# Matrix multiply with GELU on one core: a new contraction order for 32-element transpose reads, narrower transfers of B, and four row tiles of A per opening load

## The chip, the cores and the metric

The kernel runs on one core of one Trainium2 chip. The metric is the device time of one execution in microseconds (us). All runs quoted here are fast (mean granted clock 0.99 to 1.0). The times "before" in the experiments are runs of the kernel before on the same chip, in turn with the kernel under test; experiments of different calls ran on different chips, and each call has its own "before". A ratio is the mean time of one kernel's fast runs over the mean of the other's fast runs of the same rounds, so it isn't quite the ratio of the medians that stand beside it.

## The reference

```python
# a: 4096 x 4096 float32, b: 4096 x 4096 float32, output float32
x = np.matmul(a, b)
return 0.5 * x * (1 + np.tanh(np.sqrt(2 / np.pi) * (x + 0.044715 * x**3)))
```

The kernel multiplies in bf16 and accumulates in float32.

## The kernel before

A contraction of 4096 is cut into four chunks of 1024. The matmuls here take A with the contraction on the partitions (the first dimension of the kernel's tiles), so A is loaded with a cast to bf16 into a staging tile, and VectorE transposes it (one instruction of 128 x 1024, 1.98 us; the index maps below are written for blocks of 32 x 32):

```python
a_v = a.rearrange("(t mb mm) (c g r) -> t c g mm mb r", mb=4, mm=Q, g=4, r=RUN)   # Q=32, RUN=256
b_v = b.rearrange("(c p j) n -> c p j n", p=P, j=NJ)                              # P=128, NJ=8
...
def load_a(t, c):
    if c == 0:
        at[t] = at_pool.tile([P, NKT, P], BF16, name="aT", tag="aT")
    s = stage_pool.tile([P, 4, RUN], BF16, name="a16", tag="a16")       # bufs=8
    for g in range(4):
        nc.gpsimd.dma_start(out=s[g * Q : (g + 1) * Q, :, :], in_=a_v[t, c, g])
    src = s.rearrange("p mb (q j) -> p j mb q", j=NJ)
    dst = at[t][:, c * NJ : (c + 1) * NJ, :].rearrange("p j (mb q) -> p j mb q", mb=4)
    nc.vector.transpose(dst, src)
```

Partition p of B holds rows 8p to 8p+7 of a chunk, so B goes in one transfer over 128 partitions, and the transpose reads its source with a step of 8 elements. The opening works on four row tiles and two column blocks (eight accumulators) while the data arrive:

```python
for c in range(NCHK):                       # 4 chunks
    for i in range(H):                      # 4 row tiles
        load_a(i, c)                        # four transfers of 64 KB (bf16)
        for n in range(2):
            load_b(n, c, 2 * i, 2 * i + 2)  # one transfer of 256 KB each
... # 256 matmuls on these; then row tiles 4 to 7, then all other column blocks
```

After that B comes 1 MB at a time and A tile by tile, ahead of their use. GpSimd issues all loads, which also cast float32 to bf16 (260.05 MB are read from HBM, 130.06 MB are moved by their queue); SyncE issues the stores. The order in which GpSimd issues the loads is not always that of the program: in the trace of this kernel, 44 loads of A for the second eight row tiles, which the program has behind all column blocks of B, are issued from 147.7 to 209.6 us, ahead of column block 5.

## Time and profile before

| | before |
|---|---|
| time, median of 3 runs | 1799.44 us (1799.33 to 1801.78) |
| matmuls, spacing after 90 us | 8192, 0.2158 us (0.21583) |
| tensor engine's lost time: start of the last weight load less 8191 x 0.21583 | 26.1 us, all in the first 90 us |
| transposes | 128 of 1.98 us |
| opening: last packet of A and B starts at | 75.6 us |
| opening: weight load 257 starts at | 80.1 us |

The trace has one weight load, reading a 128 x 128 block of A, for each of the 8192 matmuls. Weight loads are all recorded, so the start of the 257th tells when the opening's 256 matmuls are through, and packet records tell when its 12.58 MB (counted in bf16) are. From 90 us on TensorE paces everything: no two weight loads are more than 0.22 us apart. The times of weight loads in the prediction were read 0.25 us too early against the timeline's clock; here they stand on that clock (80.1 for its 79.9).

### The profile page before, as it was taken

The page shows a single profiled execution, that of the slowest core. Times are in us where ns is not written, and L with a number is a line of the kernel's source. Part 1 is how long each engine was busy: PE and PEld are TensorE (multiplying, and loading weights), DVE is VectorE, ACT ScalarE, POOL GpSimd, SP SyncE. Part 2 cuts the span into 40 slices and gives each one's busy share as a digit, 9 for nine tenths or more (in the row PEclk, how much of TensorE's full clock was granted, in tenths as well). Part 3 has the DMA queues.
Part 4 walks back from the last instruction along what each step waited for, and adds up shares of the span by engine and source line. Part 5 has one row for each costly group of instructions (what it writes and reads, how often), then busy time and mean ns, then how long its engine had stood idle before and what let it go on. Part 6 is the DMA issues. An engine that isn't in the chain of part 4 may idle for free.

```text
span 1798.2 us, 18458 instructions
## 1 busy us (share of the span) xinstructions
PE 1765.6 (98%) x8029; PEld 801.5 (45%) x8192; DVE 248.7 (14%) x128; ACT 153.8 (9%) x257; POOL 371.5 (21%) x632
## 2 busy tenths in 40 slices
PE   7899999999999999999999999999999999999999
PEld 2344444444444444444444444444444444444444
DVE  3450300006700000000850000000090000000000
ACT  0000000000000000000000000000000000000000
POOL 8751520005810000000680000000070000000000
PEclk9999999999999999999999999999999999999999
DMA  9999994416954666520795446661090654566101
GB/s 166 193 173 223 174 190 90 98 41 95 151 104 88 129 131 134 101 70 36 115 146 113 97 97 129 135 129 42 35 135 35 135 105 87 107 135 129 42 35 42
DMA packets 206737, 198.38 MB, mean 110 GB/s; under 512 B 14144, under 2 KB 173888, under 8 KB 206656
## 3 DMA queue, kind: packets, MB, share of 16 engines
q0 software_dynamic: 169792, 130.06, 49.2%
q1 hardware_dynamic: 36864, 67.13, 10.5%
q8 instruction: 64, 1.05, 0.2%
q14 instruction: 17, 0.14, 0.0%
HBM read 260.05 MB, written 67.11 MB: 182 GB/s over the span
## 4 chain that ended last, share of the span: by engine, by line
PE 94%; DMA 3%; POOL 2%; issue 1%; DVE 0%; ACT 0%; DVEq 0%; ACTq 0%; POOLq 0%
PE acc L74 94%; DMA Bc<-in_b_dram 2%; POOL a L59 1%; DMA a<-in_a_dram 1%; POOL Bc L68 0%; DVE aT L62 0%; ACT y L81 0%; DVEq L62 0%; ACTq L81 0%; POOLq L163 0%; POOLq L59 0%
## 5 line engine op out<-in xcount | busy, mean ns | idle before, releaser
L74 PE MATMUL acc<-Bc,aT 128*128 128x512 bf16 x8029 | 1765.6, 379 | 29.0 <-DMA Bc<-in_b_dram 18.2
L74 PEld LDWEIGHTS <-aT 128*128 128x128 bf16 x8192 | 801.5, 98 | 992.6 <-issue 16.1
L62 DVE STREAM_TRANSPOSE aT<-a 128x1024 bf16<-128x1024 bf16 x128 | 248.7, 1983 | 1101.6 <-PE acc L74 965.1
L59 POOL DMA_DIRECT2D a<-in_a_dram x512 | 275.9, 553 | 452.4 <-DVE aT L62 348.1
L81 ACT ACTIVATE y<-acc 128x512 f32<-128x512 f32 x256 | 152.5, 597 | 1640.7 <-PE acc L74 1573.9
L68 POOL DMA_DIRECT2D Bc<-in_b_dram x116 | 96.0, 836 | 808.7 <-PE acc L74 593.5
L81 ACT ACT_TABLE_LOAD x1 | 1.3, 1283 | 0.7 <-PEq L163 0.7
L163 POOL MEMSET const-float32-0.0<- 128x1 f32 x1 | 0.1, 98 | 0.2 <-issue 0.2
L163 POOL MEMSET const-bfloat16-1.0<- 128x1 bf16 x1 | 0.1, 101 | 0.0
L163 POOL MEMSET const-float32-1.0<- 128x1 f32 x1 | 0.1, 98 | 0.0
L163 POOL MEMSET const-uint8-127<- 128x1 uint8 x1 | 0.1, 98 | 0.0
## 6 DMA issues: line engine op xcount, KB each, us to landing
Bc<-in_b_dram POOLq DMA_DIRECT2D x84, 1024.0 KB, 19.5
out_dram<-y SPq DMA_DIRECT2D x256, 256.0 KB, 2.1
a<-in_a_dram POOLq DMA_DIRECT2D x512, 64.0 KB, 4.0
Bc<-in_b_dram POOLq DMA_DIRECT2D x32, 256.0 KB, 5.6
```

The source lines that it names most:

```text
L59: nc.gpsimd.dma_start(out=s[g * Q : (g + 1) * Q, :, :], in_=a_v[t, c, g])
L62: nc.vector.transpose(dst, src)
L68: nc.gpsimd.dma_start(out=bc[n][:, c * NJ + j0 : c * NJ + j1, :], in_=b_v[c, :, j0:j1, n * NC : (n + 1) * NC],)
L74: nc.tensor.matmul(acc[:, :], at[t][:, kt, :], bc[n][:, kt, :], start=(kt == 0), stop=(kt == NKT - 1),)
L81: nc.scalar.activation(y[:, :], acc[:, :], ACT.Gelu_apprx_tanh)
L163: nc = _bacc.Bacc("TRN2", target_bir_lowering=False, num_devices=1)
```

## The change

Its intent is that transposes read runs of 32 adjacent elements. For that, row q of a 32-partition group g must be contraction index 256g + 32j + q, which no longer lets B go in one transfer over 128 partitions. B is split in four, and the opening's A is loaded for four row tiles at once.

```diff
-    a_v = a.rearrange("(t mb mm) (c g r) -> t c g mm mb r", mb=4, mm=Q, g=4, r=RUN)
-    b_v = b.rearrange("(c p j) n -> c p j n", p=P, j=NJ)
+    a_v = a.rearrange("(x mm) (c g r) -> c g mm x r", mm=Q, g=4, r=RUN)
+    b_v = b.rearrange("(c g j q) n -> c g q j n", g=4, j=NJ, q=Q)
...
-    def load_a(t, c):
+    def load_a(t0, nt, c):
...
-        s = stage_pool.tile([P, 4, RUN], BF16, name="a16", tag="a16")
+        s = stage_pool.tile([P, 4 * nt, RUN], BF16, name="a16", tag=f"a16_{nt}", bufs=2 if nt > 1 else 3)
         for g in range(4):
-            nc.gpsimd.dma_start(out=s[g * Q : (g + 1) * Q, :, :], in_=a_v[t, c, g])
-        src = s.rearrange("p mb (q j) -> p j mb q", j=NJ)
+            nc.gpsimd.dma_start(
+                out=s[g * Q : (g + 1) * Q, :, :], in_=a_v[c, g, :, 4 * t0 : 4 * (t0 + nt), :]
+            )
+        for t in range(t0, t0 + nt):
...
+            src = s[:, 4 * (t - t0) : 4 * (t - t0 + 1), :].rearrange("p mb (j q) -> p j mb q", j=NJ)
...
     def load_b(n, c, j0, j1):
-        nc.gpsimd.dma_start(
-            out=bc[n][:, c * NJ + j0 : c * NJ + j1, :],
-            in_=b_v[c, :, j0:j1, n * NC : (n + 1) * NC],
-        )
+        for g in range(4):
+            nc.gpsimd.dma_start(
+                out=bc[n][g * Q : (g + 1) * Q, c * NJ + j0 : c * NJ + j1, :],
+                in_=b_v[c, g, :, j0:j1, n * NC : (n + 1) * NC],
+            )
...
     for c in range(NCHK):
-        for i in range(H):
-            load_a(i, c)
+        load_a(0, H, c)
+        for j in range(0, NJ, 4):
             for n in range(2):
-                load_b(n, c, 2 * i, 2 * i + 2)
+                load_b(n, c, j, j + 4)
```

More of the change, by code (lines that the diff above doesn't have):

```diff
@@ L45 @@
     psum_pool = ctx.enter_context(tc.tile_pool(name="psum", bufs=8, space=bass.MemoryType.PSUM))
-    a_v = a.rearrange("(t mb mm) (c g r) -> t c g mm mb r", mb=4, mm=Q, g=4, r=RUN)
-    b_v = b.rearrange("(c p j) n -> c p j n", p=P, j=NJ)
+    a_v = a.rearrange("(x mm) (c g r) -> c g mm x r", mm=Q, g=4, r=RUN)
+    b_v = b.rearrange("(c g j q) n -> c g q j n", g=4, j=NJ, q=Q)
     at = {}
     bc = {}
-    def load_a(t, c):
-        if c == 0:
-            at[t] = at_pool.tile([P, NKT, P], BF16, name="aT", tag="aT")
-        s = stage_pool.tile([P, 4, RUN], BF16, name="a16", tag="a16")
+    def load_a(t0, nt, c):
+        s = stage_pool.tile([P, 4 * nt, RUN], BF16, name="a16", tag=f"a16_{nt}", bufs=2 if nt > 1 else 3)
         for g in range(4):
-            nc.gpsimd.dma_start(out=s[g * Q : (g + 1) * Q, :, :], in_=a_v[t, c, g])
-        src = s.rearrange("p mb (q j) -> p j mb q", j=NJ)
-        dst = at[t][:, c * NJ : (c + 1) * NJ, :].rearrange("p j (mb q) -> p j mb q", mb=4)
-        nc.vector.transpose(dst, src)
+            nc.gpsimd.dma_start(
+                out=s[g * Q : (g + 1) * Q, :, :], in_=a_v[c, g, :, 4 * t0 : 4 * (t0 + nt), :]
+            )
+        for t in range(t0, t0 + nt):
+            if c == 0:
+                at[t] = at_pool.tile([P, NKT, P], BF16, name="aT", tag="aT")
+            src = s[:, 4 * (t - t0) : 4 * (t - t0 + 1), :].rearrange("p mb (j q) -> p j mb q", j=NJ)
+            dst = at[t][:, c * NJ : (c + 1) * NJ, :].rearrange("p j (mb q) -> p j mb q", mb=4)
+            nc.vector.transpose(dst, src)
     def new_b(n):
@@ L139 @@
                 for c in range(NCHK):
-                    load_a(x, c)
+                    load_a(x, 1, c)
             else:
```

## The prediction

> **What bounds the kernel now.** I read the page first, for the share of each engine, then the tensor engine's idle time, then the first 90 us instruction by instruction.
>
> ```profile
> span 1798.2 us, 18458 instructions
> ...
> PE 1765.6 (98%) x8029; PEld 801.5 (45%) x8192; DVE 248.7 (14%) x128; ACT 153.8 (9%) x257; POOL 371.5 (21%) x632
> ...
> L74 PE MATMUL acc<-Bc,aT 128*128 128x512 bf16 x8029 | 1765.6, 379 | 29.0 <-DMA Bc<-in_b_dram 18.2
> L62 DVE STREAM_TRANSPOSE aT<-a 128x1024 bf16<-128x1024 bf16 x128 | 248.7, 1983 | 1101.6 <-PE acc L74 965.1
> L59 POOL DMA_DIRECT2D a<-in_a_dram x512 | 275.9, 553 | 452.4 <-DVE aT L62 348.1
> L68 POOL DMA_DIRECT2D Bc<-in_b_dram x116 | 96.0, 836 | 808.7 <-PE acc L74 593.5
> ```
>
> PE is busy 98% and idle only 29.0 us, most of it behind B's transfers. The 8192 weight loads (all recorded) give the pace: from 90 us to the end they start 0.2158 us apart with no gap over 0.25 us. So 8192 x 0.2158 = 1768 us is a floor that this change doesn't touch, and 2% faster than 1799.44 would be 1763.5, below that floor. After the last weight load (1793.75) come 4.4 us of matmul, GELU and store, also untouched. What can move is the opening: the weight load numbered 294 starts at 89.5 us, where 294 x 0.2158 = 63.5 would do, so 26 us are lost there. The timeline shows how:
>
> ```profile
> 8.22 0.59 PE L74 MATMUL acc<-Bc,aT 128*128 128x512 bf16 x1 [8.22 <-DMA Bc<-in_b_dram]
> ...
> 72.07 2.00 DVE L62 STREAM_TRANSPOSE aT<-a 128x1024 bf16<-128x1024 bf16 x1 [3.11 <-DMA a<-in_a_dram]
> 74.31 14.40 PE L74 MATMUL acc<-Bc,aT 128*128 128x512 bf16 x65 [0.67 <-DMA Bc<-in_b_dram]
> ...
> 89.78 20.46 PE L74 MATMUL acc<-Bc,aT 128*128 128x512 bf16 x92 [1.06 <-DVE aT L62]
> ```
>
> The columns are start, length, engine and operands, and what ended the idle time. VectorE's last transpose of the four opening tiles ends at 74.07; 27 of the opening's 256 matmuls are left then and the opening ends at 79.9 (weight load 257). Row tile 4 then arrives too slowly and PE waits twice more, at 84.9 and 87.9 us, 2 us together by the spacing of the weight loads.
>
> ```profile
> 20.00:30.00 10.00, 9.44 (x43) 4.00 (x41) 5.29 (x3) 0.00 (x0) 8.40 (x15) 1.00 1.28 184
> 50.00:60.00 10.00, 8.71 (x39) 3.83 (x40) 5.68 (x3) 0.00 (x0) 8.76 (x15) 1.00 1.25 187
> 100.00:110.00 10.00, 9.95 (x47) 4.50 (x47) 7.95 (x5) 1.14 (x2) 8.11 (x16) 1.00 0.99 135
> ```
>
> ```profile
> POOL a L59 <- DMA Bc<-in_b_dram: 61.9, 25, 5.7
> ```
>
> The first rows are of the table by stretch: length, then busy time of PE, weight load, VectorE, ScalarE and GpSimd, granted clock, DMA share, GB/s. In the opening the DMA engines are over-full (shares above 1: packets overlap) at 184 to 187 GB/s of bf16. It needs 4.19 MB of A and 8.39 MB of B: 12.58 MB at 187 is 67 us; with the first packet at 2.8 us, some dips and about 1.5 us of landing that is the 74 us seen. Each contraction chunk starts 17 us after the one before it (weight loads 65, 129, 193 at 27.4, 44.2, 61.3) for 64 x 0.2158 = 13.8 us of matmul. **The transfers bound the opening, PE bounds the rest.** The single line, from the list of waits, is GpSimd waiting to issue: by count of the issues each such wait is for the transfer issued eight earlier, so I take eight to be in flight at most.
>
> [...] The old transpose steps 8 bf16[...]. The trace has 1.98[...]. [...] A already goes in 32-partition transfers: I counted packets in 0.4 us steps of the opening, and steps with almost only A (512 B packets, 60 ns) move a median of 179 GB/s, steps with almost only B (1 KB, 98 ns) 197. [...] a loss of some per cent for B is possible. [...] The trace shows 0.43 us steps up to 17 us and 0.216 after; the later opening gaps, at most 2.2 us, cost no clock.
>
> **The change part by part.**
> 1. Transposes, 128 of them: [...] VectorE idles 1101 us; on the path lies only the time from landing to use in each opening chunk[...] and it counts only where A lands last.
> 2. B's order and split: the same 1 KB packets, 94,208 of them. Issues rise from 116 to 64 + 336 = 400. GpSimd's cost of one depends weakly on its descriptors (0.72 us for 256, 0.87 for 1024, 0.55 for A's 128): I take 0.55 for the opening's and 0.6 for the later. B is then 35 + 200 = 235 us against 96. Opening A is 16 issues at about 0.65, 10 us for the old 64 x 0.55 = 35. GpSimd in all: 371 - 35 + 10 - 96 + 235, about 485 us, 27% busy. In an opening chunk it is 16 x 0.55 + 4 x 0.65 = 11.4 us, inside 17 us of transfer. Eight transfers of 128 KB still are 1 MB in flight, 5.5 us of transfer.
> 3. Opening order. A chunk is now: A of all four tiles (1.05 MB, 5.6 us at 187), then B's first half for column blocks 0 and 1 (2.8 us each), then the second halves. With chunk 3's data starting near 2.8 + 3 x 17.2 = 54.4, A has landed at 61.5 and the first B piece near 64.6 (with 1.5 us of landing). If the instructions are ordered to use pieces as they come, as those of before are, each piece is 3.45 us of matmul for 2.8 us of transfer, and PE runs through: 64.6 + 13.8 = 78.4. If both column blocks must be there before it starts, 81.3. Before it was 79.9. I take 79.
> 4. Row tile 4: its loads queue directly behind B and have three staging buffers of their own, with faster transposes to free them. Three chunks should be there by 80, so I expect most of the 2 us of waits to go. Old 79.9 + 2.0 = 81.9 against new 79 + 0.5 = 79.5: 2.4 us less.
> 5. A new cost: the 3.4 us of slack per chunk, before spread over three gaps, becomes one gap. [...] 0.8 us.
>
> Sum: 1799.4 - 2.4 + 0.8 = 1797.8.
>
> **The rivals.** *B's narrow transfers are slower.* If all opening traffic ran at A's 179 instead of 187, 12.58 MB would take 70.3 us, 3 us more: 1801. [...] against it: the A steps reach 192 in their best tenth though their packets are half the size. *Block 2 of B becomes late.* It is first needed at weight load 513, 136.6 us, its last chunk 5.2 us later; in the trace its transfer starts at 116.8 and 4.19 MB at 200 GB/s last 21 us, so only some 3 us are spare. Slower issue of tiles 4 to 7 (64 x 0.55 = 35 us at least, before 44) with three staging buffers instead of eight could delay it: 2 to 5 us more, 1800 to 1803. Against it: those 44 us contain waits, and the transposes free the buffers sooner. *Something large:* GpSimd, blocked at a staging buffer, holds back B later on. It waits 348 us for VectorE in before without hurting PE; B has 55 us for 22 us of transfer, so I give this a few per cent only. *The faster transposes are the gain:* [...] Against it: chunks queue behind transfers, so only the last counts.
>
> **Range and chances.** The rivals span 1794 to 1803; I take 1794.5 to 1802 and 1797.8. Over 2% faster needs less than the floor: 0.005. Over 2% slower is 36 us more, which only a blocked B or halved bandwidth gives: 0.03.
>
> **What would show it.** [...] GpSimd near 27%; weight load 257 at 78 to 81 us; no PE gap over 0.3 us after 82; weight loads at 0.2158 apart. Opening stretches under 180 GB/s would speak for the narrow transfers; 0.43 us steps at a chunk's start for the clock; a gap near 137 to 142 for late B. PE gaps in mid-run, or transposes still near 2 us, would make the prediction wrong.

## The result, and the profile after

The changed kernel took 1796.05 us (median of 4 runs, 1795.03 to 1797.56) against 1800.16 us for the kernel before (4 runs). The ratio is 0.9977, with a 95% interval of 0.9959 to 0.9994: 4 us less, far within 2%. A repeat gave 1795.89 us and a ratio of 0.9976.

These lines are from the changed kernel's page: the shares of the engines, then the groups of instructions with busy time, mean duration and idle time before them.

```profile
span 1793.3 us, 18949 instructions
...
PE 1773.7 (99%) x8192; PEld 802.3 (45%) x8192; DVE 157.1 (9%) x128; ACT 153.8 (9%) x257; POOL 477.4 (27%) x868
...
L78 PE MATMUL acc<-Bc,aT 128*128 128x512 bf16 x8192 | 1773.7, 380 | 15.9 <-DMA Bc<-in_b_dram 14.5
L72 POOL DMA_DIRECT2D Bc<-in_b_dram x400 | 226.8, 571 | 818.0 <-PE acc L78 635.7
L57 POOL DMA_DIRECT2D a<-in_a_dram x464 | 250.4, 547 | 345.0 <-DVE aT L65 288.6
...
L65 DVE STREAM_TRANSPOSE aT<-a 128x1024 bf16<-128x1024 bf16 x128 | 157.1, 1239 | 1200.3 <-PE acc L78 686.1
```

TensorE's listed idle time fell from 29.0 to 15.9 us, but these two can't be compared: 163 matmul records are missing before and none after, and 8.3 of the 29.0 us lie after 92 us, where no two weight loads are more than 0.22 us apart. The weight loads give the fair figure below. The transposes are 0.74 us shorter each, and GpSimd issues 864 transfers instead of 628. The timeline of the changed kernel shows how the opening ends (start, length, engine, what ended the idle time):

```profile
58.75 4.62 DVE L65 STREAM_TRANSPOSE aT<-a 128x1024 bf16<-128x1024 bf16 x4 [11.20 <-DMA a<-in_a_dram]
...
63.43 46.52 PEld L78 LDWEIGHTS <-aT 128*128 128x128 bf16 x217 [0.80 <-DVE aT L65]
63.43 46.79 PE L78 MATMUL acc<-Bc,aT 128*128 128x512 bf16 x216 [0.31 <-DVE aT L65]
```

The last chunk's four transposes run in a row, and from 63.43 us TensorE never stops again. Weight load 257 starts at 76.4 us, 3.7 us earlier than the 80.1 before. The wait behind row tile 4 (weight load 295 came at 89.8 us, 1.65 us after the one before it) is gone too, which is the rest, 1.2 us, of the 5.0 us by which the lost time fell in the profiled runs (26.1 to 21.2). The mid-run pace is 0.2158 us, as before. So all of the difference lies in the opening, and the next view says where it comes from: the table by stretch for 4 to 58 us, first of the kernel before, then of the changed one (length, busy time of PE, weight load, VectorE, ScalarE and GpSimd, granted clock, DMA share, GB/s).

```profile
4.00:58.00 54.00, 42.55 (x172) 17.41 (x176) 23.91 (x12) 0.00 (x0) 45.77 (x77) 1.00 1.25 181
```

```profile
4.00:58.00 54.00, 42.38 (x173) 17.71 (x173) 13.87 (x12) 0.00 (x0) 37.26 (x67) 0.97 1.30 193
```

The same bytes flow at 193 GB/s instead of 181, and GpSimd is busy for 8.5 us less. The last opening packet starts at 70.7 us instead of 75.6. Not all of that lies in this stretch: the kernel before also had a dip to 96 and 28 GB/s from 65 to 67 us, after GpSimd stood still for 1.7 us for a reason that the profile doesn't show. The changed kernel has such a pause too (2.4 us before 60.5 us), and then a dip to 98 GB/s. The prediction had taken this rate as fixed at 187.

### The profile page after: what moved, and what is told of

Same layout as the page of the kernel before. It is cut to its first block, busy times and chain, and to the rows that moved or that the text cites. A ratio compares the mean times of both kernels' runs of the same rounds, so it can differ in the third digit from the quotient of the medians.

```text
span 1793.3 us, 18949 instructions
## 1 busy us (share of the span) xinstructions
PE 1773.7 (99%) x8192; PEld 802.3 (45%) x8192; DVE 157.1 (9%) x128; ACT 153.8 (9%) x257; POOL 477.4 (27%) x868
## 3 DMA queue, kind: packets, MB, share of 16 engines
q8 instruction: 64, 1.05, 0.2%
## 4 chain that ended last, share of the span: by engine, by line
PE 96%; DMA 2%; POOL 1%; issue 0%; DVE 0%; ACT 0%; DVEq 0%; ACTq 0%; POOLq 0%
PE acc L78 96%; DMA a<-in_a_dram 1%; POOL Bc L72 1%; POOL a L57 0%; DMA Bc<-in_b_dram 0%; DVE aT L65 0%; ACT y L85 0%; DVEq L65 0%; ACTq L85 0%; POOLq L167 0%
## 5 line engine op out<-in xcount | busy, mean ns | idle before, releaser
L78 PE MATMUL acc<-Bc,aT 128*128 128x512 bf16 x8192 | 1773.7, 380 | 15.9 <-DMA Bc<-in_b_dram 14.5
L72 POOL DMA_DIRECT2D Bc<-in_b_dram x400 | 226.8, 571 | 818.0 <-PE acc L78 635.7
L57 POOL DMA_DIRECT2D a<-in_a_dram x464 | 250.4, 547 | 345.0 <-DVE aT L65 288.6
L65 DVE STREAM_TRANSPOSE aT<-a 128x1024 bf16<-128x1024 bf16 x128 | 157.1, 1239 | 1200.3 <-PE acc L78 686.1
```

The lines of the kernel that those rows point to most:

```text
L72: nc.gpsimd.dma_start(out=bc[n][g * Q : (g + 1) * Q, c * NJ + j0 : c * NJ + j1, :], in_=b_v[c, g, :, j0:j1, n * NC : (n + 1) * NC],)
L78: nc.tensor.matmul(acc[:, :], at[t][:, kt, :], bc[n][:, kt, :], start=(kt == 0), stop=(kt == NKT - 1),)
```

## The experiments

Theory I says that the stream was slow before because A came in transfers of 64 KB, which GpSimd issues too slowly to keep the DMA engines full. Theory W says that the new order's addresses or the narrow transfers made the stream faster. Theory V says that the short transposes made the gain. "Wide" B means transfers over 128 partitions, "narrow" over 32. What GpSimd can issue is also limited in number: in the traces each issue comes after the landing of the transfer eight earlier (at least 0.28 us after it, for all 620 issues that have one in the kernel before and all 856 in the changed kernel). No run changes that limit of eight, so it is part of theory I here and not a theory of its own. Each edit is against the changed kernel unless it says otherwise. All results were correct.

### Old contraction order, narrow B (e1_old_order_narrow_b)

```diff
-            src = s[...].rearrange("p mb (j q) -> p j mb q", j=NJ)
+            src = s[...].rearrange("p mb (q j) -> p j mb q", j=NJ)
-    b_v = b.rearrange("(c g j q) n -> c g q j n", g=4, j=NJ, q=Q)
+    b_v = b.rearrange("(c g q j) n -> c g q j n", g=4, j=NJ, q=Q)
```

Expected:

> The changed kernel with the old contraction order (transposes step 8 elements, 1.98 us each) but with its loads: A of four row tiles at once, B in 32-partition transfers. If the size of the opening's A transfers is what counts (theory I: GpSimd's issue and the eight in flight kept the DMA engines short of work before), the opening's last packet starts at about 71 us as in the changed kernel (before: 75.6) and the time is 1796 to 1798. If the addresses of the new order make the transfers faster (theory W), it starts at 75 and the time is 1799 to 1801. If the transposes are the gain (theory V), the last packet starts near 71 but weight load 257 comes 3 to 4 us later than the 76.4 us of the changed kernel, and the time is 1799 to 1800.

Measured: 1797.44 us (before: 1800.42), ratio 0.9984 (0.9970 to 0.9997). The last opening packet starts at 70.5 us, weight load 257 at 80.2. The timeline of this run shows the cost of the long transposes in the last chunk:

```profile
59.57 7.64 DVE L65 STREAM_TRANSPOSE aT<-a 128x1024 bf16<-128x1024 bf16 x4 [8.26 <-DMA a<-in_a_dram]
...
67.26 2.70 PEld L78 LDWEIGHTS <-aT 128*128 128x128 bf16 x14 [1.76 <-DVE aT L65]
```

This is its stretch from 4 to 58 us:

```profile
4.00:58.00 54.00, 38.34 (x159) 16.02 (x163) 22.85 (x12) 0.00 (x0) 36.99 (x66) 1.00 1.29 192
```

The stream is as fast as in the changed kernel (192 GB/s against 193), so theory W's addresses fall. Four transposes in a row take 7.64 us here and 4.62 us in the changed kernel, and TensorE waits for the fourth until 67.3. That is where theory V is right in part: the new order is worth 1797.44 - 1796.0 = 1.4 us, given that A arrives four tiles at once (1796.0 stands for the changed kernel's 1796.05 and 1795.89. They were run at other times. Their intervals overlap with this run's). Theory V's other mark, weight load 257 later by 3 to 4 us, was met by the profiles, 80.2 against 76.4, but these are of this kernel's slowest run (1798.87) and the changed kernel's fastest (1795.03); in the changed kernel's other profile, below, it is at 78.0.

### Old contraction order, wide B (e2_old_order_wide_b)

The edit is the one above, and B's load is put back to one transfer over 128 partitions:

```diff
+    b_v = b.rearrange("(c p j) n -> c p j n", p=P, j=NJ)
-        for g in range(4):
-            nc.gpsimd.dma_start(out=bc[n][g * Q : (g + 1) * Q, ...], in_=b_v[c, g, :, ...])
+        nc.gpsimd.dma_start(out=bc[n][:, ...], in_=b_v[c, :, ...])
```

Expected:

> As the run with the old order and narrow B, but B in 128-partition transfers of 512 KB in the opening and 1 MB later, as before. Theory I: last opening packet at 69 to 71 us, GpSimd under 50% busy in the opening, 1795 to 1797. If the narrow transfers themselves were the gain (another form of theory W), the packet starts at 75 and the time is 1799 to 1801. Theory V: 1799 to 1800 by late transposes. Against the run with narrow B it gives the price of the split: within 1 us by theory I.

Measured: 1795.87 us (before: 1800.42), ratio 0.9976 (0.9963 to 0.9988), last opening packet at 68.0 us. This is the same stretch, 4 to 58 us, of this run:

```profile
4.00:58.00 54.00, 39.85 (x167) 16.70 (x171) 22.87 (x12) 0.00 (x0) 21.45 (x32) 1.00 1.32 201
```

With neither the new order nor the split, this kernel is as fast as the changed one. GpSimd is busy 21 us of 54, and the stream runs at 201 GB/s. Set beside the run with narrow B, the split costs 1797.44 - 1795.87 = 1.6 us, a little more than was allowed for. The five runs of each don't overlap (1795.18 to 1796.57, 1797.09 to 1798.87), so this cost is shown. So the new opening loads (A of four tiles at once and ahead of B, larger pieces of B) bring 4.5 us, the split takes 1.6 back, and the new order returns 1.4.

### Opening A tile by tile, ahead of B (e3_single_tile_a)

```diff
-        load_a(0, H, c)
+        for i in range(H):
+            load_a(i, 1, c)          # staging: 8 buffers
```

Expected:

> The changed kernel with its opening A loaded tile by tile again (64 KB transfers, eight staging buffers), all four tiles of a chunk ahead of B as in the changed kernel. An opening chunk is then 32 issues of about 0.55 us, 17.6 us of GpSimd, a little more than the 16 us its bytes need. Theory I: last opening packet at 76 to 80 us, weight load 257 at 81 to 85, 1800 to 1805. Theories W and V: as the changed kernel, last packet near 71 and 1796 to 1797.

Measured: 1813.36 us, ratio 1.0073 (1.0060 to 1.0085). The last opening packet starts at 87.8 us and weight load 257 at 94.7. Theory I had the direction; the size was underestimated, because I set GpSimd's 17.6 us against the stream's 16 as if they overlapped in full. They don't: from 23 to 30 us, while A is issued, the stream carries 151 GB/s, and then the tensor engine stands still, and the weight loads that follow its gaps of 7.4 and 4.4 us are 0.43 us apart instead of 0.216. Theories W and V can't explain 17 us.

### The new order alone, with the old loads (e5_new_order_old_loads)

```diff
-        load_a(0, H, c)
-        for j in range(0, NJ, 4):
+        for i in range(H):
+            load_a(i, 1, c)          # staging: 8 buffers
             for n in range(2):
-                load_b(n, c, j, j + 4)
+                load_b(n, c, 2 * i, 2 * i + 2)
```

Expected:

> The new contraction order alone: opening loads as before, one row tile and then two of the eight rows of B for both column blocks, where B has to be four transfers of 64 KB instead of one of 256 KB. That is 48 issues of about 0.55 us in a chunk, 26 us of GpSimd against 16 us of transfer. Theory I: chunks 26 us apart, last opening packet at 105 to 112 us, 1826 to 1836. Theories W and V (order or transposes are the gain): 1796 to 1800.

Measured: 1840.82 us, ratio 1.0225 (1.0211 to 1.0239), last opening packet at 116.1 us, 113 GB/s from 4 to 58 us. Time and packet are both beyond what theory I expected. With all transfers at 64 KB the opening goes at the pace of issue (GpSimd is busy 49.7 of the 54 us), somewhat worse than the sum of issue times. The parts of the change therefore can't be judged one by one: the short transposes need the split, and the split needs larger pieces and fewer transfers of A to be affordable.

### Larger narrow pieces of B in the middle (e4_whole_b_mid)

```diff
-        for j in range(0, NJ, 4):
+        step = NJ if c in (1, 2) else 4
+        for j in range(0, NJ, step):
             for n in range(2):
-                load_b(n, c, j, j + 4)
+                load_b(n, c, j, j + step)
```

Expected:

> The changed kernel, with B of opening chunks 1 and 2 in transfers of 256 KB (all eight rows of a 32-partition group) instead of 128 KB: 8 issues in place of 16 in those chunks. Issue theory: the dips of the changed kernel's stream after each block of A (as at 44 us) come from issues of 128 KB at 0.55 to 0.63 us, so they go and the last opening packet starts at 68 to 70 us (70.7 before the edit); 1794 to 1796. If the narrow transfers are slow by themselves, the stream stays at 70.7 and the time at 1796; column block 0 alone at a chunk's start may also cost a little.

Measured: 1795.43 us (before: 1800.61), ratio 0.9972 (0.9958 to 0.9985), last opening packet at 70.2 us. The dip behind chunk 2's A (at 47 us; the expectation had it 3 us too early) did go: in the two steps of 1 us from 47 us on, the packets carried 135 and 128 GB/s in the changed kernel, 177 and 186 in its repeat, and 206 and 205 here. In chunk 3, still with 128 KB, it stayed (96 to 159 GB/s from 62 to 66 us, 98 to 165 in the changed kernel), though there GpSimd had also just paused for 1.3 us without a reason shown. The time moved by 0.5 us, inside the intervals, so this run speaks for the dips hanging on the size of the pieces, but doesn't show what they cost. The packets themselves give no sign of a second cost: B's median packet takes 98 ns narrow and wide. The mean in the opening is 100 to 101 ns in these narrow runs and 98 in the wide ones, but 103 in the kernel before, which is wide too. How the 1.6 us divide stays open.

### Wide B in quarters (e6_wide_b_quarters, repeated as r_quarters)

Edit, against the second run (old order, wide B):

```diff
-        for j in range(0, NJ, 4):
+        for j in range(0, NJ, 2):
             for n in range(2):
-                load_b(n, c, j, j + 4)
+                load_b(n, c, j, j + 2)
```

Against the kernel before, this changes only the opening's A loads (four tiles at once, ahead of B) and the staging buffers. Expected:

> Old contraction order and wide B as in the second run, but B in 256 KB pieces of two rows as in the kernel before, so that against the kernel before the A of four tiles in one set of transfers ahead of B (and two staging sizes) is the only edit. Theory I (size of A's transfers): last opening packet at 68 to 69 us, 1795 to 1797. If B's larger pieces were part of the gain: 72 or later, 1798 or more.

Measured: 1794.83 us (before: 1800.61), ratio 0.9969 (0.9957 to 0.9982), last opening packet at 67.7 us. Its stretch from 4 to 58 us:

```profile
4.00:58.00 54.00, 42.10 (x172) 17.32 (x173) 22.93 (x12) 0.00 (x0) 29.64 (x44) 1.00 1.31 199
```

The expectation of the repeat:

> The run with B in wide quarters and the old contraction order again, unedited, to see whether its lead of about 1.1 us over the changed kernel (1794.83 against 1796.05 and 1795.89) holds in another call. If it does: 1794 to 1795.5, ratio 0.9969 within 0.0005, last opening packet near 67.7 us. If it was the draw of that call: 1796.

The repeat took 1794.47 us (1794.42 to 1794.57), ratio 0.9967. Its five runs all lie below every run of the changed kernel (lowest 1795.03). In the first call the five runs (1794.44 to 1795.67) overlap with the changed kernel's. This version beats the kernel before by 5.7 us, and its medians lie 1.2 to 1.4 us below the changed kernel's, with the long transposes and the old order; the two never ran in the same rounds, so the lead over the changed kernel is likely rather than shown.

### The same with single tiles (e7_single_first_wide_b)

Edit, against the run in quarters: `load_a(0, H, c)` becomes four calls `load_a(i, 1, c)`, and staging gets eight buffers. Expected:

> As the run with B in quarters, but with A of the four tiles in 64 KB transfers, still all ahead of B. It tells the order from the size. Theory I: A's 1.05 MB take 16 x 0.55 = 8.8 us at the pace of GpSimd's issue, about 120 GB/s, and B 10.2 us at 206 GB/s: 19 us a chunk, last opening packet at 77 to 79 us, 1804 to 1808. If the order (A first) made the gain, it is like the run with quarters: 1796.

Measured: 1811.30 us, ratio 1.0060 (1.0047 to 1.0072), last opening packet at 84.5 us. This is the strongest pair: the order of the loads in the program is the same as in the run in quarters, only A's transfers are 64 KB instead of 256 (with the same room for staging in the opening), and the time differs by 16.5 us. The stretch from 4 to 58 us falls from 199 to 152 GB/s:

```profile
4.00:58.00 54.00, 33.44 (x134) 14.07 (x135) 23.50 (x12) 0.00 (x0) 41.34 (x70) 0.95 1.11 152
```

GpSimd's first rows in the two timelines show the mechanism, single tiles first, then the run in quarters:

```profile
1.32 8.71 POOL L57 DMA_DIRECT2D a<-in_a_dram  x16 [0.87 <-POOLq L167]
```

```profile
1.32 2.70 POOL L57 DMA_DIRECT2D a<-in_a_dram  x4 [0.87 <-POOLq L166]
```

The same 1.05 MB takes 8.71 us to issue in 16 transfers, without a wait between them, and 2.70 us in four. That is 120 GB/s against 388, where the stream carries 199 GB/s in the run in quarters and 201 in the second run. Pace alone isn't the whole of it, since GpSimd is busy for only 41.3 of the 54 us. In the next chunk A's transfers are issued one by one as B's land, because of the limit of eight, and the rest then in a row:

```profile
21.89 0.54 POOL L57 DMA_DIRECT2D a<-in_a_dram  x1 [0.70 <-DMA Bc<-in_b_dram]
23.16 0.54 POOL L57 DMA_DIRECT2D a<-in_a_dram  x1 [0.73 <-DMA Bc<-in_b_dram]
24.45 4.81 POOL L57 DMA_DIRECT2D a<-in_a_dram  x9 [0.74 <-DMA Bc<-in_b_dram]
```

So GpSimd can't run ahead while B flows (199 GB/s from 18 to 24 us), and the burst that is left goes at the pace of issue (126 GB/s from 25 to 30 us). The kernel before put 512 KB of B behind every 256 KB of A, which may have hidden part of this. How its 181 GB/s come about is not shown in detail: GpSimd idles 8.2 of the 54 us there, 6.8 of them until a B lands, and its dip to 106 GB/s from 30 to 31 us comes with seven transfers issued and not landed. What the runs show is that larger transfers of A, loaded ahead of B, remove the loss.

### Last chunk in two halves (e8_split_last_chunk)

Edit, against the second run (old order, wide B): the last chunk is loaded as two tiles of A, B of block 0, two tiles of A, B of block 1; to make room, the four-tile staging set had one buffer instead of two.

> A try to beat both: old contraction order, wide B, A of four tiles at once, but the last opening chunk in the order two tiles of A, B of column block 0, the other two tiles of A, B of column block 1, so that less matmul is left when the stream ends. By my sum of 3.45 us of matmul for each piece of 512 KB, weight load 257 comes 2 us earlier than in the second run (76.7): 74 to 76, and the time is 1793 to 1795.5. If the slow transposes of the late tiles or row tile 4 hold it up instead, no gain: 1796.

Measured: 1799.19 us, ratio 0.9996 (0.9984 to 1.0009). It failed. The last opening packet started at 67.2 us, but chunk 2 started late (its last A packet at 46.5 us and first transpose at 47.2, where the second run has 42.4 and 42.9; that the single staging buffer delayed it is likely, since the last chunk's edit comes later). After the gaps that followed, TensorE ran at half clock from 54.8 to 59.5 us (granted clock 0.50 from 55 to 59). So my own saving of a buffer spoils this test of the idea, and it stays open.

### Pairs of tiles (e9_pairs_wide_b, e10_pairs_new_order)

Edits: the first against the second run (old order, wide B), the other against the changed kernel, both with four staging buffers for pairs.

```diff
+        for h in range(2):
+            load_a(2 * h, 2, c)
+            ...  # half of the chunk's B: quarters (e9) or narrow 128 KB pieces (e10)
```

> Second try to beat both: the run with B in quarters, but A in pairs of row tiles (128 KB transfers), the two pairs of a chunk interleaved with B's quarters as before had its single tiles. GpSimd needs 8 x 0.57 + 8 x 0.72 = 10.3 us a chunk. If a transfer of 128 KB (0.57 us to issue, so up to 225 GB/s) already keeps the stream full, the last opening packet starts at 68 to 69 us; PE begins chunk 0 earlier (weight load 65 at 28 to 30 us, 33.6 in the quarters run) and has less left at the end: weight load 257 at 74 to 76, 1793 to 1795. If 128 KB isn't enough, the stream ends at 71 or later and the time is 1796 or more.

> The same pairs in the new contraction order with its short transposes and narrow B (128 KB): 8 x 0.57 + 16 x 0.55 = 13.4 us of GpSimd a chunk. If issue pace is the limit, it is behind the pairs with wide B by 1 to 2 us: last opening packet at 70 to 72, 1794.5 to 1797. If short transposes count here, since they come twice a chunk, it is ahead: 1792.5 to 1794.

Measured: 1795.92 us, ratio 0.9976 (0.9963 to 0.9990) for wide B, and 1798.66 us, ratio 0.9991 (0.9979 to 1.0004), with a spread of 1795.74 to 1801.00, for the new order. With wide B, pairs bring most of the gain (194 GB/s from 4 to 58 us, last opening packet at 68.9 us) without loading all of A first, but no more than four tiles do, and the hoped-for 1793 to 1795 was missed (weight load 257 at 77.3 us). With narrow B they are worse than expected: GpSimd is busy 43 of the 54 us, the last packet starts at 72.7 us, and in the profiled run half clock from 70.5 to 74.7 us (granted clock 0.50 from 70.5 to 74.5) came on top.

### The changed kernel again (r_after)

> The changed kernel unedited, again, on the same chip as the two with pairs: 1796.05 as at first, within 1 us (1795 to 1797.1), weight load 257 near 76.4 and last opening packet near 70.7 us.

Measured: 1795.89 us. The last opening packet was at 70.75 us, but weight load 257 started at 78.0 us, not 76.4: the same kernel, 1.6 us later. The stretch from 63.5 to 66.5 us, first of the first profiled run, then of this one, tells why (the number after the five busy times is the granted clock):

```profile
63.50:66.50 3.00, 3.00 (x15) 1.35 (x16) 0.00 (x0) 0.00 (x0) 2.36 (x5) 1.00 1.04 123
```

```profile
63.50:66.50 3.00, 3.00 (x8) 1.07 (x9) 0.00 (x0) 0.00 (x0) 2.40 (x5) 0.50 1.01 123
```

In this execution the clock was halved at the start of chunk 3 and 8 matmuls were recorded where 15 had been. In the first one the half clock fell in chunk 2 (47.6 to 50.9 us, granted clock 0.50 from 47.7 to 50.7), where TensorE had to wait for data again before chunk 3. The runs of the changed kernel spread over 2.5 us and in this repeat over 1.6, those in quarters over 1.2 and in their repeat over 0.15 us. That the clock causes this spread is plausible but not shown: there are only two profiles of the changed kernel.

## Why the prediction was right or wrong

The time, 1796.05 us, lies inside the range, and "within 2%" was right for the reason given: 8192 x 0.2158 us was untouched, and only the opening moved. The forecast drop was 1.6 us and the measured one about 4. That the time lies inside a range of 7.5 us says little; the difference lies nearly all in step 3. The steps:

1. **Transposes.** Right in kind. How much shorter they would get was not shown by any trace at the time. Measured for 128 x 1024 bf16: 1.98 us with a step of 8 elements, 1.25 us alone and 1.155 us in a row (4.62 / 4) with runs of 32, a factor of 1.6 to 1.7; 157 us in all instead of 249. On the path they are worth 1.4 us in this kernel (first run against the changed one). The rival "the faster transposes are the gain" counts one tile in each of four chunks, 4 x (1.98 - 1.155) = 3.3 us by the measured times, and was too large.
2. **B's split and GpSimd's issue.** 226.8 us for B against 235, and 477 us for GpSimd against 485: right. The rival of slower narrow transfers was right in sign, 1.6 us, but its picture was wrong: the changed kernel's stream was not slower than the one before but faster. I counted packets again in 0.4 us steps, those with over 80% A or B. Steps of A, always narrow, carry a median of 174 GB/s before and 193 to 196 in the changed kernel; steps of B carry 200 narrow (changed kernel, first run) and 205 to 207 wide (second run, quarters). So the slow A steps in which the prediction looked for a cost of narrow transfers came from something that went with the 64 KB transfers.
3. **Opening order.** This is the term that was mis-sized: "I take 79", measured 76.4 and 78.0. Its picture of the end was right: TensorE runs through from chunk 3's start, at 63.4 us (64.6 in the prediction, where its own terms give 54.4 + 5.6 + 2.8 + 1.5 = 64.3), but A was there at 58.8 us instead of 61.5. The 1.5 us in this sum stands for landing; in the trace before, by the order of the packets, the opening's loads land 0.2 to 1.9 us after their last packet, with a median of 0.9 for A and 0.5 for B. I had called the transfers the bound at 187 GB/s and reckoned every new order with that rate. The 187 was no property of the DMA engines. It was what they got with A coming in 64 KB transfers, and 201 GB/s was there to be had (second run). The line of waits quoted in the prediction and GpSimd's 8.4 to 8.8 busy us of every 10 were signs. I read them as harmless since a chunk's issues (16 x 0.55 + 8 x 0.72 = 14.6 us) fit into 17 us, and did not ask what a burst of A's issue does when no more than eight transfers can be ahead.
4. **Row tile 4.** Right: no gap remains. It was worth 1.2 us, not the 2 us that I counted: of the two waits the one near 85 us delays nothing (weight loads 0.35 and then 0.08 us apart). The prediction's 29.0 us of idle time also holds 8.3 us that stand for missing records.
5. **The clock.** The 0.8 us put down for it were the author's estimate; no trace showed them. Right by luck, as a coin toss: none of it in one profiled run, 1.6 us in the other. The cause was not the one foreseen: no single gap of 3.4 us came, but three short ones, with weight loads 1.4, 0.9 and 1.1 us apart. After them the matmuls ran at a granted clock of 0.50, from 47.6 us in one execution and only from 63.5 us in another of the same kernel. So several short gaps in a row were followed by half clock here, and not each time: in the kernel before, weight loads 1.6, 0.7, 1.4 and 0.8 us apart between 45 and 52 us left it at 1.00.

Late B for block 2 did not happen: its last packet starts at 135.7 us, and the weight loads run on without a gap. The large rival, a blocked GpSimd, did not show either.

## What to carry to other kernels

When the DMA engines look full, ask at what pace the transfers are issued during each burst, not only on average: here 64 KB per 0.545 us of issue are 120 GB/s, the stream carried 126 in a burst of them (25 to 30 us of the run with single tiles) where it carries 200 otherwise, and with eight in flight at most GpSimd couldn't run ahead to hide it. A transfer of A of 256 KB takes only 0.64 us to issue, and with these the kernel took 16.5 us less (1794.83 against 1811.30). Judge a change that couples several edits by undoing them one by one; here a single part, larger opening loads of A ahead of B, makes more than the whole gain (5.7 us), and the split (1.6 us lost) and the new order (1.4 us won) cancel each other. When an opening leaves several idle gaps close together, allow for the tensor engine's half clock after them (here a granted clock of 0.50 from 47.7 to 50.7 us, after weight loads 1.45, 0.93 and 1.13 us apart).
